# The input projection of the retention as seven block products, with its results through DRAM

## The chip, the cores and the metric

The kernel runs as one program on one core of a Trainium2 chip. The core has five engines that run at the same time and wait for each other through semaphores: TensorE (PE, matmuls into PSUM banks of 128 x 512 float32), VectorE (DVE), ScalarE (ACT), GpSimd (POOL) and SyncE (SP), whose queue issues all DMA transfers here, in order. The metric is the device time of one execution in microseconds (us); lower is better.

## The reference, cut to what matters

One layer of a decoder on a sequence of 1024 rows with 1024 features, all in float32. `D_IN` is 6400: the combined projection gives the retention's q and k (512 columns each, 4 heads of 128), v and its gate (1024 each, 256 per head), branch B's q, k, v (1024, 128, 128), and two gates of 1024.

```
h = rms_norm(x, ln1_g)
proj = h @ w_in + b_in
rq, rk, rv, rg, aq, ak, av, gate_a, gate_b = split(proj)

rq = rotary(rq); rk = rotary(rk)
ry = head_group_norm(retention_chunkwise(rq, rk, rv), ret_norm_g)     # chunks of 128 rows
branch_a = (silu(rg) * ry) @ w_ret_out

ay = sliding_window_sink_attention(rotary(aq), rotary(ak), av, sinks)  # window 128
branch_b = ay @ w_attn_out

merged = sigmoid(gate_a) * branch_a + sigmoid(gate_b) * branch_b
x = x + merged @ w_out
h2 = rms_norm(x, ln2_g)
x = x + (silu(h2 @ w_ffn_gate) * (h2 @ w_ffn_up)) @ w_ffn_down
out = rms_norm(x, lnf_g)
```

## The kernel before

**Split products.** Float32 products are made of parts: each operand is split into a high part in the matmul's type (`hi`, an ACT copy) and a remainder (`lo`, a DVE subtraction), and each product is three matmuls, hi x hi, hi x lo, lo x hi. h is kept transposed and split in two tiles `H[0]` and `H[1]` (features 0 to 511 and 512 to 1023).

**`dense_g`** projects one block of 128 output columns: `slab` loads 1024 x 128 weights and splits them, then for each half of the rows `mm_g` does 8 x 3 = 24 matmuls 128x512 into one PSUM bank, and `evac` takes the result. It is a generator that yields after every three matmuls, so that its matmuls can be dealt out between the steps of other work. `Fill` holds a list of such generators; `fl.step(n)` runs n of their pieces.

**Stages, in the order of the program.** (1) First norm, h transposed. (2) Branch B's attention, 32 units, filled with its own q projection (`quad_q`) and 14 of the 16 column blocks of the two gates (`gate`), whose tanh goes to DRAM (`tb_d`). The unit's result overwrites its q in place, in `B`. (3) Branch B's output projection, eight `dense` blocks with names `bb`, whose gated result goes to DRAM (`mb_d`). (4) The retention: for each head h, `core(h)` runs over eight chunks in pairs (scores, states, outputs, then `gated`), filled with the head's gate (`rg_g`, two blocks) and the next head's k and q (`rk_g`, `rq_g`), or with two blocks of gate A (`ga_g`) in the last head. Between heads stand `k_transpose` and `rv_g`, the head's v: for each of 8 row chunks, 8 x 3 matmuls of 256 columns, with h as the stationary operand. (5) Branch A's output projection and the merge (`ba`), (6) w_out and the second norm, (7) the feed-forward part, already made of seven block products in place of eight (P1 to P7), with POOL making the sums of weights and DVE the sums of results.

The order on each engine is set by the program's order, a scheduler that ranks instructions, and `tc.high_priority` around weight loads. Tiles come from pools; a tile with a tag and `bufs=n` waits until the tile n before it is no longer used. The tag `wr` holds raw weights, `wh` and `wl` split ones, two buffers each. A pool that is opened where another was closed waits for that one's last uses. PSUM has the tags `acc` (3 banks), `s` and `t` (2 each) and `pv` (1).

Of the kernel before, what the change touches and what calls it, by code (L numbers as in the profile page):

```python
# [37 lines left out]
def hybrid_block(ctx: ExitStack, tc: tile.TileContext, x, ln1_g, w_in, b_in, ret_norm_g, w_ret_out,  # L38
# [20 lines left out]
    mb_d = dram.tile([8, P, S], F32, name="mb_d")  # L59
    act_d = dram.tile([7, NF // 2, P, 512], F32, name="act_d")  # L60
# [207 lines left out]
    with tc.tile_pool(name="w1", bufs=1) as w1:  # L268
# [227 lines left out]

        for n in range(8):
            def evac(half, pt):
                t = r512("ra", 2, f"tbr{n}{half}")
                nc.sync.dma_start(t, tb_d[8 + n, :, half * 512:half * 512 + 512])  # L500
                m = r512("rb", 1, f"mb{n}{half}")
                nc.vector.scalar_tensor_tensor(out=m, in0=t, scalar=1.0, in1=pt, op0=ALU.add, op1=ALU.mult)
                nc.sync.dma_start(mb_d[n, :, half * 512:half * 512 + 512], m)
            dense(w_attn_out, n * P, B, evac, f"bb{n}")


    w23 = tc.tile_pool(name="w23", bufs=1)
    pqk = w23.__enter__()
    w2c = tc.tile_pool(name="w2", bufs=1, side="right")
    w2 = w2c.__enter__()  # L510
    rtab = w2.tile([P, 2, S], F32, name="rtab")
    nc.sync.dma_start(rtab, c_rtab.rearrange("z p s -> p z s"))
    qTs, kTs, kts, vvs, rgs = {}, {}, {}, {}, {}

    def rot_g(col, dst, bc, name):
        def evac(half, pt):
            c = slice(half * 512, half * 512 + 512)
            nc.scalar.activation(dst[:, c], pt, AF.Identity, bias=bc, scale=1.0)
            xw = w2.tile([P, 512], F32, tag="tmp", bufs=2, name=f"xw{name}{half}")
            nc.sync.dma_start(xw[0:64, :], dst[64:128, c])  # L520
            nc.sync.dma_start(xw[64:128, :], dst[0:64, c])
            nc.vector.tensor_tensor(out=dst[:, c], in0=dst[:, c], in1=rtab[:, 0, c], op=ALU.mult)
            nc.vector.tensor_tensor(out=xw, in0=xw, in1=rtab[:, 1, c], op=ALU.mult)
            nc.vector.tensor_tensor(out=dst[:, c], in0=dst[:, c], in1=xw, op=ALU.add)
        return dense_g(w_in, col, H, evac, name)

    def rk_g(h):
        kTs[h] = pqk.tile([P, S], F32, tag="kT", name=f"rk{h}")
        yield from rot_g(C_RK + h * P, kTs[h], bcol[:, 4 + h:5 + h], f"rk{h}")

    def rq_g(h):
        qTs[h] = pqk.tile([P, S], F32, tag="qT", name=f"rq{h}")
        yield from rot_g(C_RQ + h * P, qTs[h], bcol[:, h:h + 1], f"rq{h}")

    def rv_g(h):

        vv = w2.tile([P, NB, 256], F32, tag="vv", bufs=1, name=f"rv{h}")
        vvs[h] = vv
        vbias = w2.tile([P, 256], F32, tag="vbias", bufs=1, name=f"vbias{h}")
        c0 = C_RV + h * 256  # L540
        nc.sync.dma_start(vbias, b_in[c0:c0 + 256].rearrange("(o d) -> o d", o=1).partition_broadcast(P)
                          .rearrange("p o d -> p (o d)"))
        nc.vector.tensor_scalar(out=vbias, in0=vbias, scalar1=rcol[:, h:h + 1], scalar2=None, op0=ALU.mult)
        wv = []
        with tc.high_priority(offset=AHEAD):
            for kk in range(2):
                raw = raw_slab([4, 256], f"rv{h}{kk}")
                nc.sync.dma_start(raw, w_in[kk * 512:kk * 512 + 512, C_RV + h * 256:C_RV + h * 256 + 256]
                                  .rearrange("(k p) n -> p k n", p=P))
                hl = hl_tiles([4, 256], f"rv{h}{kk}")  # L550
                split(raw, *hl)
                wv.append(hl)
        def part(pt, c, ks):
            o = pt[:, 0:256]
            for k in ks:
                hi, lo = wv[k // 4]
                xh = H[k // 4][:, 2 * (k % 4), c * P:c * P + P]
                xl = H[k // 4][:, 2 * (k % 4) + 1, c * P:c * P + P]
                nc.tensor.matmul(o, xh, hi[:, k % 4, :], start=(k == 0), stop=False)  # L559
                nc.tensor.matmul(o, xh, lo[:, k % 4, :], start=False, stop=False)  # L560
                nc.tensor.matmul(o, xl, hi[:, k % 4, :], start=False, stop=(k == 7))  # L561
                if k % 2:
                    yield

        for cs in ((0, 1, 2), (3,), (4,), (5,), (6,), (7,)):
            pts = [acc(f"rv{h}{c}") for c in cs]
            for ks in (range(4), range(4, 8)):
                for c, pt in zip(cs, pts):
                    yield from part(pt, c, ks)
            for c, pt in zip(cs, pts):  # L570
# [197 lines left out]
    w23.__exit__(None, None, None)  # L768

# [497 lines left out]
```

## Time and profile before

| | |
|---|---|
| median of 3 runs | 1633.66 us (1633.03 to 1634.69) |
| the profiled execution | 1633.71 us, span in the profile 1631.9 us |
| mean granted PE clock | 0.996 |
| busy: PE, DVE, ACT, POOL | 1608.7, 884.8, 673.8, 306.8 us |
| DMA | 179.12 MB, 110 GB/s on average |
| retention's k, q, v, gate, gate A's two blocks | 768 matmuls of 256 columns, 864 of 512 |
| branch B's output projection | 384 matmuls of 512 columns |

PE's busy time sums up overlapping matmuls into stretches; how long a matmul occupies PE is read from how closely one follows the other. "Idle before" in a group's row is the engine's idle time just ahead of it, with what ended it.

### The profile page before, as it was taken

The page shows a single profiled execution, that of the slowest core. Times are in us where ns is not written, and L with a number is a line of the kernel's source. Part 1 is how long each engine was busy: PE and PEld are TensorE (multiplying, and loading weights), DVE is VectorE, ACT ScalarE, POOL GpSimd, SP SyncE. Part 2 cuts the span into 40 slices and gives each one's busy share as a digit, 9 for nine tenths or more (in the row PEclk, how much of TensorE's full clock was granted, in tenths as well). Part 3 has the DMA queues.
Part 4 walks back from the last instruction along what each step waited for, and adds up shares of the span by engine and source line. Part 5 has one row for each costly group of instructions (what it writes and reads, how often), then busy time and mean ns, then how long its engine had stood idle before and what let it go on. Part 6 is the DMA issues. An engine that isn't in the chain of part 4 may idle for free.

```text
span 1631.9 us, 21378 instructions
## 1 busy us (share of the span) xinstructions
PE 1608.7 (99%) x8035; PEld 1360.0 (83%) x8035; DVE 884.8 (54%) x1636; ACT 673.8 (41%) x1335; POOL 306.8 (19%) x269
## 2 busy tenths in 40 slices
PE   8999999999999999999999998999999999999998
PEld 7888888888889898989888886888888888788886
DVE  6458767662234545555344248544444444688656
ACT  5357777761013333323222145333333333444445
POOL 2000000000000000000000025655556666300001
PEclk9999999999999999999999999999999999999999
DMA  6554424314441212121345300333333333763333
GB/s 203 162 165 117 142 71 136 104 60 129 152 136 43 67 44 65 44 65 40 122 124 169 115 1 26 110 112 102 103 97 106 109 115 98 268 261 91 97 98 122
DMA packets 142262, 179.12 MB, mean 110 GB/s; under 512 B 7819, under 2 KB 91085, under 8 KB 141134
## 3 DMA queue, kind: packets, MB, share of 16 engines
q1 hardware_dynamic: 142158, 177.75, 34.5%
q8 instruction: 63, 1.03, 0.3%
q14 instruction: 41, 0.34, 0.1%
HBM read 127.65 MB, written 45.35 MB: 106 GB/s over the span
## 4 chain that ended last, share of the span: by engine, by line
PE 91%; DVE 4%; ACT 2%; DMA 1%; issue 1%; POOL 1%; SPq 0%; POOLq 0%; DVEq 0%; ACTq 0%
PE fA L968 14%; PE fB L968 7%; PE dA L1186 6%; PE dxP L1186 5%; PE fC L968 3%; PE acc_g L139 2%; PE acc_g L140 2%; PE acc_g L141 2%; PE rv L559 2%; PE rv L560 2%; PE rv L561 2%; PE acc_rg L139 2%; PE acc_rg L140 2%; PE acc_rg L141 2%; PE acc_ba L140 2%; PE acc_bb L139 2%
## 5 line engine op out<-in xcount | busy, mean ns | idle before, releaser
L1186 PE MATMUL dA<-dwP,daP 128*128 128x512 f32 x528 | 121.4, 390 | 1.4 <-DVE dwP L123 1.4
L1186 PEld LDWEIGHTS dA<-dwP,daP 128*128 128x128 f32 x528 | 98.8, 188 | 23.4 <-DVE dwP L123 2.4
L665 POOL TENSOR_TENSOR grs<-gve,mhalf 128x2 f32<-128x2 f32 x16 | 11.2, 700 | 426.9 <-DVE gve L663 404.9
L1186 PE MATMUL dxP<-dwP,daP 128*128 128x512 f32 x396 | 90.2, 389 | 0.0
L139 PE MATMUL acc_g<-h,wh_g 128*128 128x512 f32 x224 | 87.8, 392 | 0.0
L140 PE MATMUL acc_g<-h,wh_g 128*128 128x512 f32 x224 | 87.8, 392 | 0.0
L141 PE MATMUL acc_g<-h,wl_g 128*128 128x512 f32 x224 | 87.4, 390 | 0.0
L1186 PEld LDWEIGHTS dxP<-dwP,daP 128*128 128x128 f32 x396 | 74.3, 188 | 15.4
L1026 POOL TENSOR_TENSOR xf<-xf 128x512 f32<-128x512 f32 x44 | 71.2, 1617 | 35.0 <-issue 30.3
L423 ACT ACTIVATE sc<-sc,nm 128x257 f32<-128x257 f32 (+1 forms) x128 | 62.3, 490 | 28.6 <-DVE nm L420 28.3
L559 PE MATMUL rv<-wh_rv,h 128*128 128x256 f32 x256 | 72.8, 284 | 0.0
L560 PE MATMUL rv<-wl_rv,h 128*128 128x256 f32 x256 | 72.4, 283 | 0.0
L561 PE MATMUL rv<-wh_rv,h 128*128 128x256 f32 x256 | 72.4, 283 | 0.0
L408 POOL COPY sc<-nsink 128x4 f32<-128x4 f32 x32 | 9.6, 303 | 310.8 <-PE pT L441 249.8
L979 POOL TENSOR_TENSOR xf<-xf 128x512 f32<-128x512 f32 x33 | 49.6, 1502 | 45.0 <-DVE xf L984 26.7
L420 DVE CUSTOM_DVE_ANT_0 sc<-s,amask,nsink 128x256 f32<-128x256 f32 (+1 forms) x128 | 52.9, 462 | 9.1 <-PE s L417 9.0
L989 ACT COPY xf<-fA 128x512 f32<-128x512 f32 x44 | 25.8, 588 | 76.1 <-PE fA L968 76.1
L123 DVE TENSOR_TENSOR dwP<-wd,dwP 128x512 fp32r<-128x512 f32 x77 | 54.8, 713 | 0.0
L139 PE MATMUL acc_rg<-h,wh_rg 128*128 128x512 f32 x128 | 50.9, 397 | 0.0
L140 PE MATMUL acc_rg<-h,wh_rg 128*128 128x512 f32 x128 | 50.1, 391 | 0.0
L139 PE MATMUL aq<-h,wh_aq 128*128 128x512 f32 x128 | 50.0, 391 | 0.0
L140 PE MATMUL aq<-h,wh_aq 128*128 128x512 f32 x128 | 49.9, 390 | 0.0
(640 smaller groups left out, 4465.1 us busy)
## 6 DMA issues: line engine op xcount, KB each, us to landing
act_d<-xf SPq DMA_DIRECT2D x77, 256.0 KB, 2.1
daP<-act_d SPq DMA_DIRECT2D x21, 512.0 KB, 8.2
q_d<-stg SPq DMA_DIRECT2D x8, 1024.0 KB, 4.1
q<-q_d SPq DMA_DIRECT2D x32, 256.0 KB, 5.4
wr_g<-in_w_in SPq DMA_DIRECT2D x14, 512.0 KB, 7.8
tb_d<-tb SPq DMA_DIRECT2D x28, 256.0 KB, 2.1
wr_daP<-act_d SPq DMA_DIRECT2D x14, 512.0 KB, 3.5
wd<-in_w_ffn_down SPq DMA_DIRECT2D x6, 1024.0 KB, 7.0
```

The costliest lines, as they stand in the source:

```text
L123: nc.vector.tensor_tensor(out=lo, in0=raw, in1=f32(hi), op=ALU.subtract)
L139: nc.tensor.matmul(pt, hi[:, k, :], xh, start=(k == 0), stop=False)
L140: nc.tensor.matmul(pt, hi[:, k, :], xl, start=False, stop=False)
L141: nc.tensor.matmul(pt, lo[:, k, :], xh, start=False, stop=(k == 7))
L420: nc.vector.tensor_tensor_reduce(out=sc[:, j, 0:nk], in0=pt[:, jj * 256:jj * 256 + nk], in1=mk, scale=1.0, scalar=nsink[:, 4 * g + j:4 * g ...
L423: nc.scalar.activation(sc[:, j, 0:nk + 1], sc[:, j, 0:nk + 1], AF.Exp, scale=-1.0, bias=nm[:, j:j + 1], accum_out=den[:, j:j + 1])
L559: nc.tensor.matmul(o, xh, hi[:, k % 4, :], start=(k == 0), stop=False)
L560: nc.tensor.matmul(o, xh, lo[:, k % 4, :], start=False, stop=False)
L561: nc.tensor.matmul(o, xl, hi[:, k % 4, :], start=False, stop=(k == 7))
L968: nc.tensor.matmul(pt, o[:, w, k, :], v, start=(first and k + z == 0), stop=(k == 3 and z == 2), skip_group_check=not first)
L1026: nc.gpsimd.tensor_tensor(out=o, in0=a, in1=b, op=op)
L1186: nc.tensor.matmul(banks[tt], a[:, u, c], w[:, v, :], start=(fresh and f + z == 0), stop=(f == NP - 1 and z == 2), skip_group_check=not fresh)
```

## The change

The feed-forward part's scheme of seven products is applied to the retention's projection. The projection is cut into blocks, rows in two halves, features in two halves, columns in two halves, and seven products of sums of blocks (P1 to P7) replace the eight products of blocks.

1. **v for all heads at once**: 28 steps (7 products x 4 blocks of 128 features) of 12 matmuls 128x512, on the weights `wv`, loaded during the attention. The sums of h (S1 to S4) are made here by POOL and DVE (`make_s12`, `make_s`), and kept for the rest of the projection; the sums of weights by POOL. Results are added up by DVE in `vacc`, which begins with the bias, and stored to DRAM (`v_d`).
2. **k, q, gate and two blocks of gate A**: nine pairs of column blocks, each 7 x 12 matmuls, in the order `wseq`, weights prepared two products ahead; rotary on DVE and POOL; results to DRAM (`rk_d`, `rg_d`, `tb_d`).
3. **The retention** loads k, q, v and gate of each head from DRAM; the per-head factor on v moves into `prep`. Its fill is now branch B's output projection (`bb_g`), whose input the attention stores to DRAM (`ay_d`) and which is loaded again in two tiles of 4 MB (`AY`). `k_transpose` of the next head moves into `core`, `gated(1)` of one head behind the first step of the next.
4. The tags A and B of the large tiles change places in the later stages.

```diff
@@ attention
+                if i % 4 == 0:
+                    g, b, _, Bt, jb, _ = geo(i - 1)
+                    c = slice((b // 4) * 512, (b // 4) * 512 + 512)
+                    nc.sync.dma_start(ay_d[g, :, :, c], f32(Bt[:, jb:jb + 4, c]))
+            if i == 2 * NB + 4:
+                wv = act.tile([P, 16, 512], F32, tag="B", name="wv")
...
-            dense(w_attn_out, n * P, B, evac, f"bb{n}")
@@ v
+    s23 = act.tile([P, 4, 4, 512], F32R, tag="B", name="s23")
+    s4h = ws_.tile([P, 2, 4, 512], F32R, name="s4h")
...
+        t, h = H[i % 10 - 1], slice((i // 10 - 1) * 512, (i // 10 - 1) * 512 + 512)
+        return t[:, 2 * k, h], t[:, 2 * k + 1, h]
...
+            return rvp.tile([P, 512], F32, tag="sum", bufs=4, name=name)
+        def make_s12(k):
...
+            gadd(s1, h21, h22)
+            gadd(t, l21, l22)
+            nc.vector.tensor_tensor(out=s1, in0=s1, in1=t, op=ALU.add)
+            nc.vector.tensor_tensor(out=t, in0=s1, in1=h11, op=ALU.subtract)
+            nc.vector.tensor_tensor(out=t, in0=t, in1=l11, op=ALU.subtract)
+            halves(t, *HX["P6"][k])
+            halves(s1, *HX["P5"][k])
...
+        def make_s(k, q, pr):
+            h, l = f32q(q, k)
+            t = sum_tile(f"s{pr}{k}")
+            gadd(t, h, l)
+            gsub(t, t, f32(HX["P6"][k][0]))
+            gsub(t, t, f32(HX["P6"][k][1]))
+            halves(t, *HX[pr][k])
+        VORDER = ("P1", "P2", "P6", "P5", "P7", "P3", "P4")
...
+            w = ring.tile([P, 2, 512], F32R, tag=("wh", "wl")[n % 2], name=f"v{pr}{k}")
+            split(b, w[:, 0], w[:, 1])
+            vops[n] = w
+            if pr == "P1":
+                gsub(b11, b12, b11)
+                gsub(t2, b22, b11)
+            elif pr == "P2":
+                gsub(b12, b22, b12)
+                gsub(b21, b21, t2)
...
+                while nv < min(28, pi * 4 + k + 3):
+                    vprep(nv)
...
+                        nc.tensor.matmul(banks[tt], x_[:, c], w[:, u, :], start=(fresh and k + z == 0),
+                                         stop=(k == 3 and z == 2), skip_group_check=not fresh)
+                if pr == "P1":
+                    make_s12(k)
+                elif pr == "P2":
+                    make_s(k, 22, "P7")
+                elif pr == "P6":
+                    make_s(k, 12, "P3")
...
+                    nc.vector.tensor_tensor(out=o, in0=banks[tt], in1=o, op=ALU.add)
+                    if pr in ("P2", "P7", "P3", "P4"):
+                        nc.sync.dma_start(v_d[:, t, z * 512:z * 512 + 512], o)
@@ pairs
+    AY = [act.tile([P, 8, 1024], F32R, tag="B", name="ay0")]
+    for g in range(2):
+        nc.sync.dma_start(f32(AY[0][:, 4 * g:4 * g + 4, :]), ay_d[g])
...
+    nc.sync.dma_start(rtab, c_rtab.rearrange("z p s -> p z s"))
+    cols = [C_RK, C_RQ, C_RK + 256, C_RQ + 256] + [C_RG + 256 * h for h in range(RH)] + [C_GA]
...
+    wseq = [(0, "P2"), (1, "P2"), (0, "P1"), (1, "P1"), (0, "P6"), (0, "P5"), (0, "P7"), (1, "P6"), (0, "P4"), (0, "P3"),
...
+        if j < 4:
+            if other is None:
+                nc.scalar.activation(r, pt, AF.Identity, bias=bias, scale=1.0)
+            else:
+                nc.vector.scalar_tensor_tensor(out=r, in0=pt, scalar=bias, in1=other, op0=ALU.add, op1=ALU.add)
+            xw = wtile("xw", 2, f"xw{j}{half}{y}")
+            nc.sync.dma_start(xw[0:64, :], r[64:128, :])
+            nc.sync.dma_start(xw[64:128, :], r[0:64, :])
+            nc.vector.tensor_tensor(out=r, in0=r, in1=rtab[:, 0, c], op=ALU.mult)
+            nc.gpsimd.tensor_tensor(out=xw, in0=xw, in1=rtab[:, 1, c], op=ALU.mult)
+            nc.vector.tensor_tensor(out=r, in0=r, in1=xw, op=ALU.add)
+            nc.sync.dma_start(rk_d[ct, :, c], r)
...
+    for i, (j, pr) in enumerate(wseq):
+        wprep_to(i + 3)
+        wproduct(j, pr)
@@ retention
+    AY.append(act.tile([P, 8, 1024], F32R, tag="B", name="ay1"))
...
+        return dense_g(w_attn_out, n * P, AY, evac, f"bb{n}")
+    def load_k(h):
+        kTs[h] = w2.tile([P, S], F32, tag="kT", name=f"rk{h}")
+        nc.sync.dma_start(kTs[h], rk_d[4 + h])
...
-        yield 8
+        yield 4
+        yield None
         gated(1)
...
+    fl = Fill([bb_g(n) for n in range(8)])
```

**Where the change moves instructions.** DVE, at v. Before, the additions of v's results (`rv`) stand between the rotary of q and the split of the next weights (`wl`):

```order
L524 TENSOR_TENSOR rq_4534<-rq_4534,xwrq_4599 128x512
L571 SCALAR_TENSOR_TENSOR rv_4621<-rv_4637,rcol,vbias_4622 128x256
L571 SCALAR_TENSOR_TENSOR rv_4621<-rv_4638,rcol,vbias_4622 128x256
L608 TENSOR_TENSOR vl_4860<-rv_4621,vh_4859 128x512
L571 SCALAR_TENSOR_TENSOR rv_4621<-rv_4639,rcol,vbias_4622 128x256
```

DVE at v now, from P2's third weight block on (`vP22` is the split block 2 of P2, `sP70` the sum for block 0 of P7, which POOL makes, `s23` and `s4h` hold its halves):

```order
L127 TENSOR_TENSOR vP22_4097<-wv_2832,vP22_4097 128x512
L518 TENSOR_TENSOR s23_3947<-sP70_4114,s23_3947 128x512
L127 TENSOR_TENSOR vP23_4120<-wv_2832,vP23_4120 128x512
L518 TENSOR_TENSOR s23_3947<-sP71_4137,s23_3947 128x512
L127 TENSOR_TENSOR vP60_4143<-wr_vt20_3961,vP60_4143 128x512
L518 TENSOR_TENSOR s23_3947<-sP72_4158,s23_3947 128x512
L127 TENSOR_TENSOR vP61_4164<-wr_vt20_3961,vP61_4164 128x512
L518 TENSOR_TENSOR s23_3947<-sP73_4179,s23_3947 128x512
```

Splits of the weights that PE needs next now alternate with halves of sums that come from POOL, and this goes on to the third weight block of P5.

SP's queue, where v's weights and the rotary table are loaded before (`mb_d` and `tbr` are stores and loads of branch B's projection, `xwrk` the halves of k exchanged for the rotary):

```order
L548 DMA wr_rv_4625<-in_w_in 128x4x256
L503 DMA mb_d<-mb_4421 128x512
L503 DMA mb_d<-mb_4451 128x512
L548 DMA wr_rv_4631<-in_w_in 128x4x256
L512 DMA rtab<-in_c_rtab 128x2x1024
L520 DMA xwrk_4496<-rk_4463 64x512
```

SP's queue now, from the last stores of v to the first weights of the pairs (`wp_4565` is the second half of pair 0's weights, the operand of its P2):

```order
L629 DMA v_d<-vacc 128x512 x8
L634 DMA ay_4556<-ay_d 128x4096 x2
L629 DMA v_d<-vacc 128x512 x4
L638 DMA rtab<-in_c_rtab 128x2x1024
L646 DMA wp_4565<-in_w_in 128x4x256
L646 DMA wp_4569<-in_w_in 128x4x256
```

Two transfers of 2 MB stand ahead of the last four stores of v, and those ahead of the table and the weights.

PE in the retention before, around one head's second pair of chunks (`u` states, `acc_rg` the gate's projection as fill):

```order
L141 MATMUL acc_rg_1_4953<-h_107,wl_rg_4871 128x512
L613 MATMUL u_4963<-vh_4941,kt_4605 128x256
L614 MATMUL u_4963<-vl_4942,kt_4605 128x256
L615 MATMUL u_4963<-vh_4941,kt_4606 128x256
L613 MATMUL u_4963<-vh_4941,kt_4605 128x256
L614 MATMUL u_4963<-vl_4942,kt_4605 128x256
L615 MATMUL u_4963<-vh_4941,kt_4606 128x256
L139 MATMUL acc_rg_1_4953<-h_107,wh_rg_4870 128x512
L140 MATMUL acc_rg_1_4953<-h_107,wh_rg_4870 128x512
```

PE in the retention now, in head 0 (`y` outputs, `acc_bb` branch B's projection, `kTT` the transposes of head 1's k):

```order
L819 MATMUL y_6187<-sth_6152,qh_6115 128x256
L143 MATMUL acc_bb_0_6357<-ay_4556,wh_bb_6353 128x512
L144 MATMUL acc_bb_0_6357<-ay_4556,wh_bb_6353 128x512
L820 MATMUL y_6187<-stl_6153,qh_6115 128x256
L821 MATMUL y_6187<-sth_6152,ql_6116 128x256
L819 MATMUL y_6284<-vh_6216,smh_6105 128x256
L819 MATMUL u_6245<-vh_6216,kt_5907 128x256
L145 MATMUL acc_bb_0_6357<-ay_4556,wl_bb_6354 128x512
```

The fill stands in smaller pieces in heads 0 and 1, and in heads 2 and 3 in pieces of 9 to 12 as before; 67 of its 384 matmuls stand ahead of the first `kTT`.

More of the change, by code (lines that the diff above doesn't have):

```diff
@@ L513, in hybrid_block, with bb_g @@
+    YG = [None, None]
     qTs, kTs, kts, vvs, rgs = {}, {}, {}, {}, {}
-    def rot_g(col, dst, bc, name):
+    def bb_g(n):
         def evac(half, pt):
             c = slice(half * 512, half * 512 + 512)
[L518 to L570, printed above, removed]
-                nc.vector.scalar_tensor_tensor(out=vv[:, c, :], in0=pt[:, 0:256], scalar=rcol[:, h:h + 1],
-                                               in1=vbias, op0=ALU.mult, op1=ALU.add)
@@ L700, in core @@
         scores(1)
+        if more:
+            load_k(h + 1)
         prep(4)
```

308 lines of the change are left out of this document (226 added, 82 removed).

## The prediction

> **What bounds the kernel now.** I read the page first: its busy times and its chain.
>
> ```profile
> PE 1608.7 (99%) x8035; PEld 1360.0 (83%) x8035; DVE 884.8 (54%) x1636; ACT 673.8 (41%) x1335; POOL 306.8 (19%) x269
> PE 91%; DVE 4%; ACT 2%; DMA 1%; issue 1%; POOL 1%; SPq 0%; POOLq 0%; DVEq 0%; ACTq 0%
> ```
>
> TensorE (PE) is the bound almost everywhere, so taking matmuls away pays in full where nothing else comes to the front. Next, the price of a matmul, from the groups of PE and from the chain in order of time (start, length, what):
>
> ```profile
> L559 PE MATMUL rv<-wh_rv,h 128*128 128x256 f32 x256 | 72.8, 284 | 0.0
> L139 PE MATMUL acc_rg<-h,wh_rg 128*128 128x512 f32 x128 | 50.9, 397 | 0.0
> 562.95 0.87 PE kTT L580 x8
> 586.86 0.89 PE rs L621 x8
> 1036.72 2.72 PE fA L968 x12
> 1473.95 29.92 PE dA L1186 x132
> ```
>
> The group means (284 and 397 ns) would price a 256-column matmul at 0.72 of a 512-column one. They are latencies of overlapping matmuls. The rate is in the chain: 2.72/12 = 29.92/132 = 0.2267 us per 512 columns; and between 563.82 (end of kTT) and 586.86 stand only the 192 v matmuls of one head, 0.120 us each. A narrow matmul costs half of a wide one: widening alone gains little.
>
> Then PE's own waits, to see what the retention leaves idle (us in total, times, longest), and the retention's rows in the chain:
>
> ```profile
> PE fC L968 <- DVE xf L865: 4.6, 1, 4.6
> PE lnT L195 <- DVE h L201: 2.7, 2, 1.6
> ...
> PE s L416 <- DVE nm L420: 0.3, 1, 0.3
> 507.75 0.89 PE rs L621 x8
> 522.88 0.89 PE rs L621 x8
> ```
>
> No wait in the retention is listed. From 508.64 to 522.88 (14.24 us) PE has 45 fill matmuls (10.20) and 33 narrow ones (3.96): 0.1 us is left. Fills of 9 to 12 matmuls between two dependent steps suffice there.
>
> **The change, part by part.**
>
> *Matmuls.* Removed: v, 768 x 0.120 = 92.2 us; 18 column blocks of 48 matmuls, 864 x 0.2267 = 195.9. Added: v, 7 x 48 = 336 x 0.2267 = 76.2; nine pairs, 756 x 0.2267 = 171.4. Branch B's 384 only move. All on the path: **-40.5 us**.
>
> *The v products: POOL in front of PE.* POOL had next to nothing to do here; now it makes 48 sums of 128x512 (16 on weights, 8 in make_s12, 24 in make_s).
>
> ```profile
> L1026 POOL TENSOR_TENSOR xf<-xf 128x512 f32<-128x512 f32 x44 | 71.2, 1617 | 35.0 <-issue 30.3
> L979 POOL TENSOR_TENSOR xf<-xf 128x512 f32<-128x512 f32 x33 | 49.6, 1502 | 45.0 <-DVE xf L984 26.7
> 985.94 1.28 POOL L875 TENSOR_TENSOR xf<-xf 128x512 f32<-128x512 f32 x1
> 992.64 1.67 DVE L874 TENSOR_TENSOR xf<-xf 128x512 f32<-128x512 f32 x1
> 993.73 1.72 POOL L814 TENSOR_TENSOR wr_f<-wrx_f,wr_f 128x512 f32<-128x512 f32 x1
> L123 DVE TENSOR_TENSOR dwP<-wd,dwP 128x512 fp32r<-128x512 f32 x77 | 54.8, 713 | 0.0
> L122 ACT CAST dwP<-wd 128x512 fp32r<-128x512 f32 x77 | 47.3, 615 | 4.8 <-PE dA L1186 4.8
> L1206 DVE TENSOR_TENSOR x<-dA,x 128x512 f32<-128x512 f32 x16 | 10.5, 686 | 0.9 <-PE dA L1186 0.8
> ```
>
> Such a sum takes 1.28 us alone and 1.72 beside DVE, which then needs 1.67 instead of 0.71; I take 1.6, between the means of the two long groups. The Trainium skill (SBUF — State Buffer, Who interferes with whom) says that a DVE instruction with two SBUF inputs and a POOL one that reads SBUF lock each other out for a whole instruction. By that rule a sum behind a DVE operation would cost up to 1.28 + 0.71 = 2.0 us, 17 us more over 42 of them; the trace shows 1.72.
>
> Let S be the first v matmul. The order puts twelve weight sums first. Six can run ahead of S; the seventh needs the third weight block's split, whose ring slot the attention's last gate block frees at S, and lands at S + 1.4 (0.62 + 0.71). From there POOL has 42 sums: 42 x 1.6 = 67.2, ending at S + 68.6. PE can't run past it, since on DVE and ACT the splits of the weight blocks of P2, P6 and P5 stand in turn with the halves of the sums that POOL makes: the split of P5's third block stands behind the last of them. After the last sum come its halves and that split, four PSUM additions (4 x 0.69), the fourth split, and PE's last blocks of P5: about 10.5 us. Then P7, P3 and P4 run at PE's pace, 3 x 10.88 = 32.6. The stage ends at S + 111.7 against 76.2: **+35.5 us**. With 1.28 a sum it is +22, with 1.74 +41.
>
> *From v to the pairs: a 4 MB load in front.* E is v's last matmul. On SP's queue the first half of branch B's activations (ay0, 2 x 2 MB) goes out when the last v weight is split, about E - 9.4, ahead of the last four v stores, the rotary table and the weights that the first pair product needs; table and weights lie where vacc lay and wait for its stores.
>
> ```profile
> 1398.51 6.36 SPq L1047 DMA_DIRECT2D wd<-in_w_ffn_down  x4
> 1404.97 2.45 SPq L1056 DMA_DIRECT2D daP<-act_d  x1
> 1417.71 0.62 ACT L122 CAST daP<-daP 128x512 fp32r<-128x512 f32 x1 [1.28 <-DMA daP<-act_d]
> 1400.00:1420.00 20.00, 18.94 (x83) 14.99 (x82) 11.17 (x13) 7.74 (x14) 9.12 (x6) 1.00 1.00 374
> act_d<-xf SPq DMA_DIRECT2D x77, 256.0 KB, 2.1
> wr_bb<-in_w_attn_out SPq DMA_DIRECT2D x8, 512.0 KB, 3.9
> rtab<-in_c_rtab SPq DMA_DIRECT2D x1, 1024.0 KB, 6.3
> ```
>
> Here 512 KB issued behind 5 MB is used only 12.7 us later, at 374 GB/s in all (last column): loads queue. So: 4.2 MB = 11.2 us plus 2.1 to land, E + 3.9; v stores 1.05 MB, E + 6.7; issue, then table and weights, 1.57 MB in 4.2 plus 2.1, E + 13.5; split 1.3: PE resumes at E + 14.8. Without the queueing it is E + 10.5; with the table's and weights' rows one after the other (6.3 + 3.9), E + 18.2. A long pause also slows PE's clock (last three columns of the window: clock, DMA share, GB/s):
>
> ```profile
> 990.00:1000.00 10.00, 7.91 (x26) 6.01 (x26) 9.90 (x8) 3.97 (x6) 10.00 (x6) 0.83 0.00 1
> 992.06 4.62 PE L968 MATMUL fC<-a,t_0P 128*128 128x512 f32 x12 [4.65 <-DVE xf L865]
> ```
>
> After 4.65 us of waiting twelve matmuls took 4.62 instead of 2.72: 1.9 more. Together **+16.7 us**; no filler stands between v's last product and the pairs' first.
>
> *Inside the pairs.* DVE, per pair of 19 us: 7 splits, 3 sums, 8 rotary operations at 0.7 to 0.8, 14 us; POOL 8 x 1.6 = 13: both fit. But each rotation waits for two transfers, as before:
>
> ```profile
> L522 DVE TENSOR_TENSOR rk<-rk,rtab 128x512 f32<-128x512 f32 x8 | 5.5, 693 | 13.6 <-DMA xwrk<-rk 13.4
> ```
>
> 1.7 us each on DVE, with splits now two products (5.4 us) ahead. Bounds: 0, and half of 16 x 1.7 = 14; nearer to 0 for the lead: **+4**.
>
> *Into the retention.* The second 4 MB (ay1) and then k, q, v of head 0 land about 19.5 us after the last pair product by the same sums; 67 of branch B's matmuls (15.2 us), k's transposes and the scores cover 18. **+2**, bounds 0 and 8 (no overlap of the two halves of ay1).
>
> *In the retention.* Per head 78 fill matmuls remain of 192; steps with 9 to 12 between them cost nothing (above), those of heads 0 and 1 with 3 to 5 lack about 0.5 us each, and each head now loads 3.1 MB of k, q, v and gate. Bounds 0 and 36 steps x 0.5 = 18; nearer to 0, since half of the steps keep their fill: **+4**.
>
> *Costed at nothing:* 8 MB of ay stores and 4 MB of v weights in the attention, which moves 118 GB/s with DMA at 0.39; the next group's q is read four units after that load, 8.9 us each (the two transposes below). If that cover fails it is 4.2 MB at 374 GB/s, 11 us.
>
> ```profile
> 212.91 0.87 PE pT L441 x8
> 221.82 0.87 PE pT L441 x8
> 100.00:500.00 400.00, 399.08 (x2057) 337.75 (x2056) 236.18 (x626) 218.11 (x564) 9.33 (x30) 1.00 0.39 118
> ```
>
> **Sum.** -40.5 + 35.5 + 16.7 + 4 + 2 + 4 = +21.7 on the profiled execution's 1633.71 us (span 1631.9, 1.8 around it; the median 1633.66 is the same): **1655 us**.
>
> **Rivals.** *A, faster:* POOL doesn't hold PE in v. For it: in the FFN POOL is busy with the same kind of sums and PE hardly waits. Against: there it makes 7 sums per 19 us of products, here 48 per 76, 78 us of work at 1.6. It decides if v's wait is under 35.5 - 21.7 = 13.8 us; with none the time is 1620. *B, the loads are hidden:* if ay0 doesn't delay the stores and weights and the clock holds, 6 us less, 1649; still slower. *C, the clock:* some 14 blocks of v between P2 and P5 each follow a short wait; were all at the slow pace of the row above (4.62), up to 14 x 1.9 = 27 us come on top, 1682. Against it: POOL's pace of 4.8 us per block already leaves room. The Trainium skill (TensorE: Matmul & The Clock Gate, What's actually happening) has the clock halve after an idle window of some 3.4 us; by that rule the bursts here, idle for about 2 us at a time, would mostly stay fast. *D, thin fill:* retention and rotations at their upper bounds add 24 us, 1679. *E, even:* POOL at 1.28 with the short load gap: 1655 - 13.5 - 6 = 1636.
>
> **Numbers.** My case with B: 0.60 (1640 to 1672). A: 0.15. C: 0.07. D: 0.10. E: 0.08, split evenly over slower and within 0.2% (3.3 us, about what a measurement tells from no change). Slower 0.60 + 0.07 + 0.10 + 0.04 = 0.81, same 0.04, faster 0.15. The range leaves out half of A and the ends of C and D: 1627 to 1682.
>
> **What would show it.** PE busy falls by some 40 us; in v, PE waits for DVE and ACT splits whose own waits name POOL, 35 us in all between P2 and P5, none in P7, P3, P4; a gap of about 15 us before the first pair product that ends on a load; the window there shows clock below 1. I am wrong if POOL ends before P6 starts, if v takes under 90 us, or if the waits lie in the retention.

## The result, and the profile after

The changed kernel takes **1683.42 us** (median of 4 runs, 1681.62 to 1685.4) beside 1633.38 (1633.03 to 1634.69) for the kernel before on the same chip: ratio **1.0305, 95% interval 1.0287 to 1.0323**. The prediction said slower, which it is, but 1655 us, with 1682 as its upper end: the sum forecast 21.7 us of loss and there are 50. Three of the runs below had one execution far outside the rest (4109, 5672 and 1777 us); their times here are medians of their other executions. Lines L.. of the kernel after are those of its own file, and those of an experiment those of its own.

The page of the kernel after: busy time of PE, the chain by engine, the granted clock in 40 slices.

```profile
PE 1596.8 (95%) x7495; PEld 1322.6 (79%) x7495; DVE 990.3 (59%) x1736; ACT 719.1 (43%) x1431; POOL 456.0 (27%) x369
PE 77%; DVE 7%; POOL 5%; DMA 5%; ACT 3%; issue 3%; SPq 0%; POOLq 0%; ACTq 0%; DVEq 0%
PEclk9999999997989999989999999999999999999999
```

PE issues 540 matmuls fewer and is busy only 12 us less: where the granted clock is low (0.88 in the v stage below), a matmul counts longer. Its share of the chain fell from 91% to 77%; DVE, POOL and DMA now hold parts of the path. What PE waited for in the v stage, in the pairs and in the retention (us in total, times, longest):

```profile
PE vP L614 <- DVE vP L127: 15.8, 1, 15.8
PE va L614 <- DVE vacc L627: 5.0, 2, 3.5
PE va L614 <- DVE vP L127: 4.6, 4, 1.6
PE va L614 <- ACT vP L126: 3.7, 1, 3.7
...
PE wC L726 <- ACT w0P L126: 15.7, 1, 15.7
PE wB L726 <- DVE r L697: 4.0, 2, 2.1
...
PE u L819 <- ACT vh L840: 6.2, 3, 2.3
PE y L819 <- ACT smh L517: 3.1, 1, 3.1
```

The three stages in windows (start and end; then length, busy time of PE, PEld, DVE, ACT and POOL with counts, granted clock, DMA share, GB/s): v, then the pairs, then the retention up to branch A's first matmul.

```profile
378.07:492.40 114.33, 85.31 (x337) 66.45 (x335) 80.25 (x85) 25.41 (x43) 64.27 (x42) 0.88 0.31 108
508.19:692.48 184.29, 179.06 (x759) 145.95 (x760) 101.65 (x122) 68.74 (x114) 79.89 (x52) 0.97 0.41 128
692.48:851.40 158.92, 146.50 (x805) 123.65 (x804) 108.46 (x262) 67.64 (x132) 11.64 (x16) 0.96 0.54 180
```

With the prices of the prediction (0.2267 us for 512 columns, 0.120 for 256, 0.87/8 for 128, the transposes and scores) the length of each stage splits into matmuls at full rate and loss:

| stage | full rate | took | lost | forecast |
|---|---|---|---|---|
| attention | | +3.2 against before | 3.2 | 0 |
| v, 336 wide | 76.2 | 114.3 | 38.1 | 35.5 |
| v to pairs, with the slow first 24 matmuls | | 15.8 + 2.4 | 18.2 | 16.7 |
| pairs, 756 wide | 171.4 | 184.3 - 2.4 | 10.5 | 4 |
| retention, 384 wide, 264 narrow, 160 of 128 columns | 136.1 | 158.9 | 22.8 | 2 + 4 |

The losses from v to the retention are 89.6 us where 62.2 were forecast. The matmuls of this stretch went from 424.2 to 383.7 us, the 40.5 of the prediction. -40.5 + 89.6 + 3.2, plus 0.5 in later stages, less 1.1 that the kernel before lost in the same stretch, is the 51.7 between the two spans.

In v, 29.1 of the 38.1 us are the waits listed above; the other 9.0 are matmuls at the lower clock. The retention's loss lies mostly in its first half. Windows that begin about where each head does:

```profile
713.40:747.50 34.10, 28.32 (x145) 23.71 (x145) 23.54 (x60) 13.36 (x28) 2.79 (x4) 0.85 0.51 168
747.50:781.50 34.00, 31.71 (x178) 26.87 (x179) 27.30 (x65) 17.09 (x35) 2.54 (x4) 0.95 0.52 172
781.50:815.00 33.50, 32.46 (x194) 27.96 (x193) 26.14 (x65) 16.17 (x32) 2.85 (x4) 1.00 0.54 178
815.00:852.00 37.00, 35.67 (x203) 30.21 (x202) 27.28 (x68) 16.59 (x32) 3.46 (x5) 1.00 0.32 109
```

They hold 63, 70, 84 and 96 of branch B's matmuls. At full rate, and up to branch A at 851.4, they lose 10.2, 5.6, 1.8 and 2.7 us; the entry before them (692.48 to 713.35) loses 2.6.

The chain in order of time shows how v ends and the pairs begin (start, length, what):

```profile
440.37 1.23 POOL sP L511
...
444.65 4.28 PE va L614 x11
448.93 10.88 PE vP L614 x48
459.81 10.88 PE va L614 x48
...
481.57 8.85 PE va L614 x39
...
490.44 2.74 DVE vacc L627 x4
...
493.20 7.71 DMA v_d<-vacc
...
501.48 5.89 DMA wp<-in_w_in
...
508.19 7.86 PE wC L726 x24
```

From 406 to 441.6 the path is POOL's row of sums; the last of them is shown. Behind a last slow block four whole products (48 matmuls, 10.88 us each) follow at full pace; the prediction had three. Then the chain leaves PE for additions, stores and weights.

### The profile page after: what moved, and what is told of

Same layout as the page of the kernel before. It is cut to its first block, busy times and chain, and to the rows that moved or that the text cites. A ratio compares the mean times of both kernels' runs of the same rounds, so it can differ in the third digit from the quotient of the medians.

```text
span 1683.6 us, 20974 instructions
## 1 busy us (share of the span) xinstructions
PE 1596.8 (95%) x7495; PEld 1322.6 (79%) x7495; DVE 990.3 (59%) x1736; ACT 719.1 (43%) x1431; POOL 456.0 (27%) x369
## 4 chain that ended last, share of the span: by engine, by line
PE 77%; DVE 7%; POOL 5%; DMA 5%; ACT 3%; issue 3%; SPq 0%; POOLq 0%; ACTq 0%; DVEq 0%
PE fA L1164 14%; PE fB L1164 7%; PE dA L1382 6%; PE dxP L1382 5%; PE wA L726 4%; PE fC L1164 3%; PE acc_g L143 3%; PE acc_g L144 3%; PE acc_g L145 3%; PE wB L726 2%; PE acc_ba L145 2%; PE acc_ba L144 2%; PE acc_ba L143 2%; PE wo L1111 2%; PE wo L1110 2%
## 5 line engine op out<-in xcount | busy, mean ns | idle before, releaser
L1327 POOL TENSOR_TENSOR rs_f<-tot,mhalf 128x1 f32<-128x1 f32 x8 | 7.9, 992 | 196.7 <-DVE tot L1324 196.7
L511 POOL TENSOR_TENSOR wr_f<-wr_f 128x512 f32<-128x512 f32 x22 | 33.8, 1539 | 78.6 <-DVE t_4P L127 9.5
L143 PE MATMUL acc_bb<-ay,wh_bb 128*128 128x512 f32 x128 | 51.5, 402 | 1.2 <-ACT wh_bb L126 1.2
L145 PE MATMUL acc_bb<-ay,wl_bb 128*128 128x512 f32 x128 | 51.2, 400 | 0.0
L144 PE MATMUL acc_bb<-ay,wh_bb 128*128 128x512 f32 x128 | 51.1, 399 | 0.0
L143 PE MATMUL aq<-h,wh_aq 128*128 128x512 f32 x128 | 50.1, 392 | 0.6 <-ACT wh_aq L362 0.6
L126 ACT CAST daP<-daP 128x512 fp32r<-128x512 f32 x42 | 26.1, 622 | 56.2 <-PE dxP L1382 26.7
```

The lines of the kernel that those rows point to most:

```text
L143: nc.tensor.matmul(pt, hi[:, k, :], xh, start=(k == 0), stop=False)
L144: nc.tensor.matmul(pt, hi[:, k, :], xl, start=False, stop=False)
L145: nc.tensor.matmul(pt, lo[:, k, :], xh, start=False, stop=(k == 7))
L511: nc.gpsimd.tensor_tensor(out=o, in0=a, in1=b, op=ALU.subtract)
```

## The experiments

The kernel before read 1633.0 to 1634.0 us (medians) beside all of them. "Theory A" is in each the reading of the prediction or of the runs so far.

### Is it the sums that hold v?

**v as plain products, sums still on POOL (v_dense).**

```diff
-        VORDER = ("P1", "P2", "P6", "P5", "P7", "P3", "P4")
+        GR = [(1, 0), (1, 1), (0, 0), (0, 1)]      # half of the rows, half of the columns
+        # per group 8 blocks of 12 matmuls; weights split as they are, no gsub on weights
+        # make_s12, make_s (for the pairs) after every second block; S1 for P5 last
```

> v for all heads stays one stage at the same place, but as plain products: 4 x 8 x 12 = 384 matmuls of 512 columns, 87.1 us at 0.2267, each weight block split as it is, no weight sums. The 36 sums of activations that the pairs need stay on POOL, in step with the products, and nothing in v waits for them. Theory A (v's 38 us of loss are POOL's sums, and DVE's halves of them, standing in front of PE): v takes 87 to 90 us instead of 114.3, the kernel 1683.4 - 26 = 1657 (1654 to 1661). Rival B (the loss lies in the splits, the clock or the port that DVE and POOL share, whatever waits for the sums): v still takes over 100 us and the kernel stays above 1668.

Measured: 1691.31 us, ratio 1.0351 (1.0336 to 1.0367). Theory A fails: nothing in v needs a sum, and v takes 120.2 us for 87.1 of matmuls. PE's waits in it, and DVE's splits of weights between 384 and 442 us:

```profile
PE v L611 <- DVE v L127: 12.1, 7, 5.4
PE v L611 <- ACT v L126: 7.3, 3, 2.9
...
L127 DVE TENSOR_TENSOR v<-wv,v 128x512 fp32r<-128x512 f32 x8 | 12.2, 1520 | 4.2 <-ACT v L126 4.2
```

PE waits for splits of weights (POOL makes 40 sums here, where the expectation counts 36). They stand in DVE's queue among the halves of POOL's sums, and each takes 1.52 us on average, not 0.69.

**P4 third instead of last (p4_early).**

```diff
-        VORDER = ("P1", "P2", "P6", "P5", "P7", "P3", "P4")
+        VORDER = ("P1", "P2", "P4", "P6", "P5", "P7", "P3")    # P4 begins afresh in the banks that P2 held
```

> The product P4 needs no sum of activations; here it is the third of v instead of the last, into banks of its own, with four more PSUM additions. Theory A (POOL's chain of 42 sums ends about 63 us after v's first matmul whatever PE does, and three products then follow it at PE's pace instead of four): v 10.9 us shorter, less about 1 for the additions, kernel 1673 to 1675. Rival B (PE is held by its own splits and clock, not by the end of the sums): no change, 1681 to 1685.

Measured: 1682.80 us, 1.0306 (1.0288 to 1.0323): no change, so theory A fails here too. PE's waits in v:

```profile
PE vP L614 <- DVE vP L127: 23.9, 2, 15.8
PE vP L614 <- DVE vacc L627: 9.7, 1, 9.7
```

P4 needs no sum, but its weights and the additions that empty its banks of P2's results go through DVE, behind halves that wait for POOL. Behind the wait of 9.7 us five whole products follow instead of four. So what holds PE is DVE's queue.

**The same sums on DVE (v_dve).**

```diff
-            gadd(s1, h21, h22)          # nc.gpsimd; likewise every gadd and gsub of the v stage
+            vadd(s1, h21, h22)          # nc.vector
```

> The sums of the v stage (weights and activations) on DVE instead of POOL; nothing else. In the changed kernel's trace a DVE operation with two SBUF inputs takes 0.68 us while POOL is idle and 1.65 to 1.77 while POOL makes sums, and a sum on POOL 1.25 or 1.6 to 1.7: the two take turns. Theory A (v's 38 us are this port shared by POOL and DVE, which also holds the splits of the next weight blocks in DVE's queue): DVE alone needs 86 operations at 0.62, 53 us, up to the last half of the sums, against 66.6 now; v takes about 102 us instead of 114, kernel 1670 to 1674. Rival B (PE waits for the sums' own chain of three or four dependent steps, on whatever engine): v stays at 110 or more, kernel above 1679.

Measured: **1663.06 us**, 1.0182 (1.0167 to 1.0198), 20.4 us less and below both ranges; v takes 96.4 us, where theory A had 102. First the window of v in this kernel, as above; then from groups of DVE and POOL (busy, mean ns of one) two of the kernel after between 384 and 442 us and one of this kernel:

```profile
377.60:474.00 96.40, 85.50 (x337) 65.60 (x335) 77.39 (x127) 26.06 (x43) 0.00 (x0) 0.93 0.36 128
```

```profile
L518 DVE TENSOR_TENSOR s<-sP,s 128x512 fp32r<-128x512 f32 x4 | 7.1, 1770 | 0.0
...
L627 DVE TENSOR_TENSOR vacc<-va,vacc 128x512 f32<-128x512 f32 x4 | 2.6, 685 | 0.0
...
L511 POOL TENSOR_TENSOR sP<-sP,s 128x512 f32<-128x512 f32 x13 | 20.0, 1545 | 0.8
```

```profile
L517 DVE TENSOR_TENSOR sP<-sP,s 128x512 f32<-128x512 f32 x16 | 10.7, 688 | 0.0
```

DVE took over 42 operations and its busy time in v *fell*, from 80.25 us for 85 to 77.39 for 127. Beside POOL a DVE operation on two SBUF operands takes up to 1.77 us instead of 0.69, while an addition that reads one operand from PSUM stays at 0.685. Sums on POOL were no help that came in addition: the two engines took turns, one sum and one DVE operation in about 1.68 us (between 406 and 415 us DVE's operations start 1.68 to 1.69 us apart, with five sums of POOL in the same 8.5 us). The Trainium skill (SBUF — State Buffer, Who interferes with whom) says just this of DVE instructions with two SBUF inputs and POOL, and that one with at most one SBUF input doesn't contend; the trace agrees with both. By its lock for a whole instruction a turn is estimated at 1.28 + 0.69 = 1.97 us; the 1.68 measured is less, and the measurement decides.

**Plain products and sums on DVE (v_dense_dve).** The two edits together.

> v as plain products (384 matmuls of 512 columns, 87.1 us), and the sums that the pairs need on DVE instead of POOL. With them on POOL this v stage took 120 us, with PE waiting 20 us for weight splits. Theory A (shared port, and splits that stand behind the sums in DVE's queue): DVE alone has some 130 operations of 0.62 in v, 81 us, under PE's 87: v 88 to 94 us, kernel 1657 to 1664. Rival B (the splits of plain products can't keep up in themselves): v above 105, kernel above 1674.

Measured: 1659.68 us, 1.0158 (1.0141 to 1.0175). v takes 87.2 us, PE never waits in it. With POOL out of v the plain products beat the seven, whose v still takes 96.4: 11 us more of matmuls, but no weight sums and half the PSUM additions. The kernel gains 3.4 us of these 9.2; the pairs behind them take 188.0 us here and 184.2 in v_dve, with POOL still in them.

### The gap before the pairs

**The 4 MB load later, in the program (ay_late).**

```diff
-    AY = [act.tile(...)]; two loads of ay0          # ahead of rtab and wload_pair
+        if i == 8:                                   # in the loop over wseq
+            AY.append(act.tile(...)); two loads of ay0
```

> The 4 MB load of the first half of branch B's activations is issued after the ninth product of the pairs instead of ahead of the table and the first pair's weights. Theory A (the 4 MB queue in front of v's last stores and of the weights): the 15.7 us gap before the first pair product falls to about 10.5, as the prediction worked out without the queueing; kernel 1677 to 1679. Rival B (the gap is the chain of additions, store, freed space, load, each with its own latency; the 4 MB cost nothing): gap 14 to 16, kernel 1681 to 1684.

Measured: 1681.41 us, 1.0295 (1.0279 to 1.0310), gap 14.4 us. But SP's queue shows the load where it was:

```profile
483.53 0.81 SPq L753 DMA_DIRECT2D ay<-ay_d  x2
491.44 2.36 SPq L629 DMA_DIRECT2D v_d<-vacc  x4
```

The edit moved the load in the program, not in the queue, so this run says nothing on the queueing.

**The load really behind the first weights (ay_behind).**

```diff
+            with tc.issue_after(last load of wload_pair(1)):
                 two loads of ay0
```

> As ay_late, where the 4 MB load had kept its place in SP's queue ahead of v's last stores; now it stands behind the table and the first pairs' weights in that queue, and nothing else moves. Theory A (the prediction's: 4 MB queue ahead of the stores and weights): the gap of 15.7 us falls to about 10.5 and the kernel to 1677 to 1679. Theory B (each link of the chain, additions, stores, space, weights, split, has its own latency, and the 4 MB cost little): gap 13 to 15.7, kernel 1681 to 1684.

Measured: 1678.07 us, 1.0273 (1.0257 to 1.0289), and PE's wait there:

```profile
PE wC L726 <- ACT w0P L126: 10.4, 1, 10.4
```

The prediction gave E + 10.5 without the queueing. With the load in front, this wait is 15.7 us in the kernel after and 14.4 to 15.3 in four runs that leave v and the queue behind it as they were (ay_late, no_rot, fill_double, loads2). So the 4 MB in front of stores and weights cost 4.0 to 5.3 us, and 10.4 are the chain through `vacc`'s space.

**Table, weights and weight sums clear of that space (early_w).**

```diff
-    rtab = wp.tile([P, 2, S], F32, name="rtab")
+    rtab = wv[:, 0:4, :].rearrange(...)       # dead after P5; the first two pairs' weights in wv[:, 4:8]
-                wtms[j] = wp.tile([P, 4, P], F32, tag="tt", ...)
+                wtms[j] = we.tile(...)        # a pool opened ahead of vacc's; ay0 loaded after pair 4
```

> Rotary table and second weight halves of the first two pairs go into parts of the v weights' tile that are dead after the product P7, the weight sums into space of their own, and the load of ay0 therefore goes out behind the fifth pair. So nothing that the first pair product needs waits for the space of vacc. Theory A (the 15.7 us gap is a chain: last additions 2.7, stores 6 to 8, the space freed, weights 6, split 0.6): the gap falls under 3 us and its 2 us of slow clock go too; kernel 1665 to 1669. Rival B (the load of the weights is late for the DMA engines, which hold 4 MB and the stores): gap still above 9, kernel above 1676.

Measured: **1664.05 us**, 1.0192 (1.0177 to 1.0207), 19.4 us less. The first product of the pairs, kernel after and this one:

```profile
L726 PE MATMUL wC<-h,w0P 128*128 128x512 f32 x12 | 5.1, 607 | 15.7 <-ACT w0P L126 15.7
```

```profile
L728 PE MATMUL wC<-h,w0P x12: 389/389/389, 492.4 to 494.9; 128*128 128x512 f32 x12
```

It starts where v ends, with no wait and at 389 ns each, the duration at full clock, instead of 607.

### The pairs

**No rotation (no_rot).**

```diff
-            xw = wtile("xw", 2, ...); two transfers; r * cos, xw * sin, r + xw
             nc.sync.dma_start(rk_d[ct, :, c], r)
```

> Leaves out the rotation of q and k (both transfers of xw, two multiplications and an addition); the rest stays. The pairs take 184 us for 171.4 of matmuls. Theory A (DVE, in order, waits in the rotation for the transfers and for POOL, so that PSUM banks of wB are read late, and the two slow spells follow): the two waits and the spells at 570 and 593 us go, 7 to 8 us; kernel 1674 to 1677. Rival B (weight splits and sums set the pace of the pairs): no more than 3 us less, kernel above 1680.

Measured: 1673.77 us, 1.0247 (1.0232 to 1.0262), 9.6 us less; the two waits for the rotation are gone, and the pairs take 175.0 us. What such a wait cost in the kernel after: one of them, and the clock behind it (window of 2 us, columns as above).

```profile
570.45 4.61 PE L726 MATMUL wB<-s4h,w2P 128*128 128x512 f32 x12 [2.10 <-DVE r L697]
```

```profile
571.00:573.00 2.00, 2.00 (x6) 1.54 (x6) 0.59 (x1) 0.00 (x0) 1.59 (x1) 0.50 0.94 302
```

Behind 2.1 us of waiting the clock was 0.50, and twelve matmuls took 4.61 us instead of 2.88. But the length of a wait doesn't decide it. In fill_double (below) PE waits at the same two places, 2.09 and 2.04 us, and runs on at full pace once and slowly once:

```profile
L726 PE MATMUL wB<-s4h,w2P x12: 389/391/499, 569.7 to 572.3; 128*128 128x512 f32 x12
L726 PE MATMUL wB<-s4h,w3P x12: 397/628/628, 592.4 to 596.6; 128*128 128x512 f32 x12
```

The traces of the kernel after and the experiments hold 21 waits of 1.8 to 2.1 us in the pairs; 11 were followed by slow matmuls and 10 were not. What decides it is open.

The rotation is at fault, but this run leaves open which part of it, transfers or POOL; the next does not.

### All repairs so far (combo)

```diff
  v_dense_dve and early_w, and in the pairs:
-                gsub(b11, b12, b11) ...; nc.gpsimd.tensor_tensor(out=xw, in0=xw, in1=rtab[:, 1, c], op=ALU.mult)
+                vsub(b11, b12, b11) ...; nc.vector.tensor_tensor(out=xw, in0=xw, in1=rtab[:, 1, c], op=ALU.mult)
```

> The changed kernel with the three repairs that the runs so far point to: v as plain products with the pairs' sums on DVE (1659.7 alone), table, first weights and weight sums clear of vacc's space (19.4 us alone), and the pairs' weight sums and rotation on DVE too, so that POOL is idle from v to the retention. Theory A (the losses are separate and add up): 1683.4 - 23.7 - 19.4 = 1640, less 0 to 7 for the pairs: 1633 to 1641. The retention's 23 us stay, so it should not beat the kernel before. Rival B (they share a cover, and the next wait appears): above 1645.

Measured: **1629.55 us**, 0.9975 (0.9965 to 0.9985): 0.25% faster than the kernel before, and 3 us better than the best expected. The windows of the pairs and of the retention:

```profile
466.60:639.20 172.60, 171.42 (x756) 141.66 (x755) 111.15 (x172) 67.57 (x111) 0.00 (x0) 1.00 0.52 166
639.20:794.40 155.20, 143.62 (x807) 120.53 (x805) 108.21 (x262) 67.74 (x132) 11.65 (x16) 0.99 0.56 184
```

The pairs take 172.6 us for 171.4 of matmuls with the rotation and its transfers in place. In early_w, which moves the same loads but leaves POOL in the pairs, they take 180.1. So most of their loss was POOL's part in them, not the transfers; whether the turns that POOL and DVE take or DVE's waits for POOL's product weigh more wasn't tried. The retention keeps its loss, 155.2 us for 136.1, as expected.

### The retention

**The fill doubled (fill_double).**

```diff
+            for again in range(2):
                 yield from mm_g(pt, w, X, half * 512)
-            fl.step(n)
+            fl.step(2 * n)
```

> Branch B's 384 matmuls in the retention are issued twice (the first set is overwritten), two sets per step: 384 more of 0.2267 = 87.1 us if none of it falls into idle time. The retention of the changed kernel takes 158.9 us from the last pair product to branch A's projection for 136 us of matmuls at full rate. Theory A (the 22.9 us are too few independent matmuls between dependent steps, with the waits and the slow clock that follow): 15 to 20 of the 87 disappear, kernel 1751 to 1756, waits of PE in the retention under 3 us. Rival B (the 22.9 us are what interleaved narrow matmuls and transposes cost in themselves, or another engine's pace): under 6 disappear, 1765 to 1771.

Measured: 1750.68 us, 1.0716 (1.0698 to 1.0733): 67.3 us more for 87.1 us of extra matmuls, so 19.8 fall into idle time. The last pair product and the first of branch A (ns min/median/max, first and last start):

```profile
L726 PE MATMUL wB<-s4h,w8P x12: 389/389/389, 688.9 to 691.4; 128*128 128x512 f32 x12
```

```profile
L143 PE MATMUL acc_ba<-yg,wh_ba x128: 389/389/478, 916.9 to 1003.4; 128*128 128x512 f32 x128
```

The retention takes 225.3 us for 223.1 of matmuls: of 22.8 us lost, 2.2 are left. So with enough fill between the dependent steps the loss goes. The longer stage also gives the loads of the heads more time; the next run moves these loads alone.

**The next heads' loads earlier (loads2).**

```diff
+    own = act.tile([P, 8, S], F32, tag="A", name="own")      # k, q, v, gate of head 1
     load_k(0) ... load_g(0); k_transpose(0)
+    load_k(1) ... load_g(1)
+        if h == 0: load_k(2) ... load_g(2)                    # once head 0 is done
```

> In the changed kernel's retention, head 1's k, q, v and gate are loaded into a free 32 KB slot of their own ahead of head 0, and head 2's as soon as head 0 is done; head 3's are loaded late as before. Theory A (what PE lacks at the head changes is the loads: three waits of 2 us for the first halves of v, each behind a transfer of 7.7 to 9.6 us): the waits at the second and third head go, 4 to 6 us, kernel 1677.5 to 1679.5. Rival B (too few independent matmuls in all: what is not waited for here is waited for at the next dependent step): under 2 us, kernel above 1681.

Measured: 1678.97 us, 1.0279 (1.0265 to 1.0293), 4.4 us less. In the kernel after the chain goes through loads at the head changes, and at the first head the dependent steps stand bare behind one:

```profile
703.00 9.57 DMA rv<-v_d
712.59 0.73 ACT vh L840
...
738.96 7.72 DMA rv<-v_d
```

```profile
718.71 0.58 PE L819 MATMUL y<-vh,smh 128*128 128x256 f32 x1 [3.12 <-ACT smh L517]
...
719.30 0.63 PE L143 MATMUL acc_bb<-ay,wh_bb 128*128 128x512 f32 x1
```

In loads2 the waits for `vh` are gone from the list, and the retention takes 150.9 us, against 155.1 to 158.9 in the kernel after, p4_early and ay_late, which all have the same retention. So the late loads are 4 to 8 us of its loss, a fifth to a third; the rest are dependent steps with too little between them, and matmuls of 0.63 us (0.43 apart) behind such waits.

**Both (combo_loads).** combo with the loads of loads2.

> combo (1629.6) with the earlier loads of loads2, which took 4.4 us alone. Theory A (separate losses): 1624 to 1627. Rival B (in combo the fill is consumed elsewhere, and the dependent steps take what the loads gave back): 1628 to 1630.

Measured: **1624.05 us**, 0.9946 (0.9934 to 0.9959). The two gains add up; the retention still takes 152.5 us for 136.1.

### Taking less of the change

**v alone, as plain products, in the kernel before (wide_v).**

```diff
-            run(rv_g(h + 1))        # 192 matmuls of 256 columns per head
+    # behind the bb blocks: 4 groups x 8 blocks x 12 matmuls 128x512 -> v_d; load_v(h) per head
```

> The kernel before, with one edit: v for all heads as one stage of plain products behind branch B's projection (384 matmuls of 512 columns, 87.1 us, instead of 768 of 256 columns, 92.2), through DRAM to the heads; k, q and the gates stay in the retention, 192 wide fill matmuls per head as before. No sums of activations at all. Theory A (a stage of plain products at full pace, thick fill): 5.1 us less, 1627 to 1630. Rival B (the loads of v at the head changes or the entry into the retention cost that much again): 1632 to 1637.

Measured: 1630.81 us, 0.9989 (0.9980 to 0.9998): between the two theories, and less than the 0.2% that the prediction took for no change. The stage takes 87.0 us, as priced; of the 5.1 us 2.2 remain in the total. Where the others went wasn't taken apart.

**v alone, in seven products, sums during branch B's projection (win_v).**

```diff
+    for n in range(8): dense(w_attn_out, ..., f"bb{n}"); make_6 / make_s of one or two blocks   # on DVE
+    VORDER = ("P1", "P2", "P6", "P3", "P7", "P5", "P4")      # raw blocks loaded per product, weight sums on DVE
```

> The kernel before, with v for all heads in seven products (336 matmuls, 76.2 us instead of 92.2), but the sums of activations for P6, P7 and P3 on DVE during branch B's projection, which stays where it was and runs 87 us with DVE nearly idle; the weight sums and those for P5 on DVE during v; k, q and the gates stay in the retention as its fill. Theory A (the products pay once nothing waits for sums, POOL stays out and the fill stays thick): DVE has some 110 operations of 0.62 in v, 68 us, under PE's 76: 16 us less, up to 5 lost to DVE's order and to late loads: 1618 to 1624. Rival B (DVE's queue holds PE in v as it does with POOL's sums in it): over 12 us lost, above 1629.

Measured: 1626.39 us, 0.9957 (0.9943 to 0.9970). The one wait of PE from v to branch A, the window of v, and that of the retention behind it:

```profile
PE vP L631 <- ACT vP L123: 4.8, 1, 4.8
```

```profile
461.80:545.80 84.00, 79.17 (x337) 65.00 (x336) 64.43 (x103) 20.38 (x32) 0.00 (x0) 0.96 0.84 280
545.80:792.40 246.60, 246.60 (x1289) 210.52 (x1288) 145.07 (x308) 99.59 (x177) 11.36 (x16) 1.00 0.31 88
```

7.8 of the 16 us are lost in v; here blocks are loaded several times (280 GB/s). The wait of 4.8 us is for a load: the chain runs through a transfer of 11.21 us of weights for P2, issued at 465.65, behind the last loads of the bias. The matmuls behind it were slow. The retention, with 192 fill matmuls per head, is busy for all of its 246.6 us, although it too loads v from DRAM at each head. The result lies between the two theories.

## Why the prediction was wrong

*Matmuls, -40.5:* right. The price came from the chain's spacing, and the stages add up with it.

*The v products, +35.5:* 38.1. The size and the place are right (POOL ends after P6, PE waits for splits between P2 and P5, none in P7, P3, P4), the reason half right, and that the size came out is partly luck. The prediction saw that DVE's queue puts splits behind the halves of sums, and saw 1.67 for DVE beside POOL, but priced only POOL's row. Two errors cancel: POOL ended 63.5 us after S, not 68.6, and P5 came whole behind it, which the prediction had nearly done by then. What v_dve adds: the sums cost that much because they were on POOL. The 9.0 us of slow matmuls within the 38.1 had no term in the sum.

*From v to the pairs, +16.7:* 15.8 and 2.4 for the clock. Right in size: 10.4 without the 4 MB against 10.5 forecast, and 14.4 to 15.7 with them against 14.8. The 1.9 for the clock sets a row (4.62) against a chain (2.72); row against row it is 4.62 against 2.88, so 1.7.

*Inside the pairs, +4:* 10.5. The bounds 0 and 14 held; the choice near 0 "for the lead" failed. The prediction checked that DVE's 14 us and POOL's 13 fit into 19 each, and did not ask whether they can run side by side, though its own row said 1.67 beside 0.71.

*Into and in the retention, +2 and +4:* **22.8, the step that failed most.** The entry is right: 2.6 against 2. What failed is the +4 inside the retention, which measured about 20. Its rule from the kernel before, that 9 to 12 fill matmuls between two dependent steps cost next to nothing, held: from 789.6 us on the pieces are of 9 to 12, the clock is 1.00, and 4.3 of 61.8 us are lost. Mis-sized were the steps with less. Ahead of 789.6 the pieces are of 1 to 10 matmuls, mostly 1 to 4, and heads 0 and 1 lost 10.2 and 5.6 us. At the prediction's own 0.5 us for each of 36 steps, half of them thin, they would have lost 9, not 4. The 15.8 measured are 0.9 for each of these 18: besides the bare steps there are late loads (4 to 8 us by loads2) and matmuls at a lower clock (0.85 and 0.95 in these heads). And the 78 fill matmuls per head are an average: the heads got 63, 70, 84 and 96, since 67 went ahead of the first. The upper bound, 18, was the better guide.

*Attention at nothing:* 3.2 us, between 150 and 185 us, where PE's listed waits grow from 0.5 to 2.2 us and the order of the units' work differs. No run took it apart.

*Rivals.* A is refuted: v waited. C is not what happened: the clock cost v 9.0 us within the forecast size, not 27 on top of it. v's bursts behind waits of 0.6 to 1.6 us mostly ran at full pace; those behind 15.8, 3.5 and 3.7 us, and the ones right after the last two, were slow. One of each kind:

```profile
408.30 5.76 PE L614 MATMUL vP<-vP,h 128*128 128x512 f32 x13 [15.77 <-DVE vP L127]
...
431.68 3.06 PE L614 MATMUL va<-vP,s 128*128 128x512 f32 x12 [1.04 <-DVE vP L127]
```

D, thin fill and rotations at their bounds, 1679, had the mechanism that decided, with a chance of 0.10. B is refuted by ay_behind and by the slow clock behind the gap, E by the result.

*The range.* The rivals were counted one at a time. Two terms went towards their upper bounds together, the pairs and the retention: with 14 and 18 for them the sum is D's 1679, and most of what is still missing are the attention's 3.2 us and v's 2.6. With all terms at their bounds it is 1695. The two may have a common root, which no run shows as one: work moved onto engines and loads that the prediction took to be free, in places where PE had no other matmuls. "I am wrong if the waits lie in the retention" was the right warning.

## What to carry to other kernels

Before work is given to an idle POOL, see what DVE does at that moment: here, where both read SBUF, 42 sums on POOL cost more than the same sums on DVE. Count what a change takes away from under other work: the retention's dependent steps had 192 wide fill matmuls per head between them and 78 on average were left, fewest in the first heads, and about 20 us of the saving went there. When several unknown terms are bounded, ask whether one cause would push them the same way, and let the range reach to where they go together.

## What the runs showed of the hardware

DVE and POOL, both on SBUF operands, got through one operation each in about 1.68 us, against 0.69 and 1.28 alone. The granted clock fell to 0.50 behind a wait of only 2.1 us, and the matmuls behind it cost 1.7 us more; the Trainium skill (TensorE: Matmul & The Clock Gate, What's actually happening) speaks of an idle window of about 3.4 us, and here the wait was shorter. Waits of the same length left the clock full about as often (10 of 21), and behind most waits of about 1 us in v it stayed up too (1.04 us, then twelve matmuls in 3.06). A 4 MB load issued 8 us ahead delayed a chain of small transfers by 4.0 to 5.3 us.
